# Six projections of two attentions: float32 matmuls from one copy of x in place of split products

## The chip, the core and the metric

The kernel runs on one core of a Trainium2 chip, as one launch. The metric is the device time of an execution in microseconds (us), the median of several runs. Before the change three runs took 1376.7, 1376.79 and 1377.83 us. The engines are TensorE (PE in the profile, its weight loads PEld), VectorE (DVE), ScalarE (ACT), GpSimd (POOL) and SyncE (SP), whose queue issues nearly all weight transfers.

## What is computed

Two transformer blocks on 256 tokens of 1024 features. Only the start of the first block matters here: the input is normalised and modulated, multiplied by one wide weight matrix, and the columns are shared out between a softmax attention ("fox") and a delta-rule recurrence ("rwkv").

```python
mod = silu(c) @ ada_w + ada_b                    # six vectors: sh1, sc1, g1, sh2, sc2, g2
h = rms_norm(x, norm1_g) * (1 + sc1) + sh1       # the modulated x: 256 x 1024
z = h @ w_in
y_fox  = fox_mixer(z[..., :FOX_COLS], ...)       # q, k, v, g: 512 columns each, 8 heads, and small gates
y_rwkv = rwkv7_mixer(z[..., FOX_COLS:], ...)     # r, k, v: 512 columns each, and low-rank parts
x = x + g1 * (concat(y_fox, y_rwkv) @ w_out)
# then a mixture of 64 experts (6 a token), and a second block of four mixers, cross attention and a gated FFN

def rwkv7_mixer(zr, mu, ...):
    zr = zr + mu * (shift_prev(zr) - zr)         # every column mixed with the token before
    r, k, v, wd, ad, gd = split_cols(zr, RWKV_SPLITS)
    ...
    o = wkv7_scan(r, decay, k, v, -kk, kk * a)   # a 64x64 state for each of 8 heads
```

## The kernel before the change

Activations lie feature-major: 128 partitions, and for each of 8 chunks of 128 features the 256 tokens. A projection of 256 output features ("step" below) is one weight tile `w` of 128x2048 (1 MB) and, for each of two halves of 128 outputs, eight products that accumulate in PSUM over the eight chunks.

There are two ways to make such a step. `gemm` (line 358) multiplies float32 weights and a float32 operand directly: 16 matmuls, each of which the profile shows as two records. `gemm3` (line 372, through `mm3`, line 383) first splits: a weight piece of 128x512 is cast to the format fp32r (`wh`, line 308 on VectorE or line 310 on ScalarE) and the remainder `wl` is subtracted on GpSimd (line 325), four pieces to a step. The operand is split once, into `xh` and `xl`. Then three fp32r matmuls (`wh` with `xh`, `wh` with `xl`, `wl` with `xh`) stand for each product, 48 to a step, one record each. The table `HD` (line 35) says which of the casts VectorE makes: all of them in the delta rule's steps (streams "0" and "1"), every second one in the other attention's ("g"); ScalarE makes the rest.

`phase_a` (line 520) makes everything up to the experts. Its first loop computes the modulation chunk by chunk (`ada`), writes the modulated x in place into the tiles `x0` and splits it into `xh` and `xl`. In the same loop it already makes four early projections, the delta rule's k among them. Then eight streams, written as generators, are woven together by the string `ORDER` (line 33): each letter advances one stream by a step. "0" and "1" prepare the two halves of the delta rule's heads (`rwkv_prepare`; its projections come from `krv`, k from the early work, r and v by `gemm3`), "g" is `fox_in` twice (four steps a half: k, q, v, g) and then the second block's memory, "a" the rest of the modulation (`po<-w,cz` in the profile, one weight tile and four matmuls a step), "c" the gates, "f" the softmax attention, "r" the recurrence, "w" the output projection.

A scheduler then places the woven instructions in one fixed order for each engine; an engine goes through its own in that order and waits where an operand, or the buffer that it writes, is not ready. Things that bind the steps to each other are:

- the ring of three 1 MB weight slots (`RING`, line 22; `weights`, line 289): a load waits until the tile three loads earlier has been read for the last time, by the last split of a `gemm3` step or by the last matmul of the others;
- two PSUM banks of each kind ("mm" for projections, "ps" for the delta rule), which the evictions on ScalarE and VectorE give back;
- VectorE's order. In the delta rule's preparation it makes the scaled keys (`kk`, `AR`, `BK`), masks the 64x64 blocks that TensorE multiplies from them (`LT<-ps`), then solves the triangular systems row by row (15 rounds of a shuffle, a product `rowj` and a sum `MC`).

`KQVG` is a set of eight 128x512 buffers, empty until `fox_in` of the first half takes four, that of the second half four more; the input x, loaded again for the residual, takes the first four over.

Of the kernel before, what the change touches and what calls it, by code (L numbers as in the profile page):

```python
# [9 lines left out]
F32 = mybir.dt.float32  # L10
# [3 lines left out]
AF = mybir.ActivationFunctionType  # L14
OP = mybir.AluOpType
# [3 lines left out]
T = 256  # L19
# [12 lines left out]
NG = 3  # L32
ORDER = "00a11101a111a0a0aa0gacc0gagagfgrafgragrfagrarfgarfrarafrargfrgrfgrfgrgrgfrgrgfrgfrgrfgrgrfgrgrfgrgfgrfrwrwwwwwww"
ALT = {}
HD = {'0': 1, '1': 1, 'g': 2}
LAG = 2
EP = 0
early_pool = lambda k: EP and k % EP == 0
# [227 lines left out]
class Prog:  # L266
# [242 lines left out]
    def phase_a(self):  # L509
        nc = self.nc  # L510
        ctx = ExitStack()
        with ctx:
# [3 lines left out]
            fb = self.pool("foxA", bufs=1, ctx=ctx)  # L516
# [20 lines left out]
            ps = self.ps("ps")  # L537
# [18 lines left out]
            xh = fb.tile([128, NK, T], F32R, tag="xh", name="xh")  # L556
            xl = fb.tile([128, NK, T], F32R, tag="xl", name="xl")
            gs = fb.tile([128, 8], F32, name="gs1")
            x = lambda k: (xh[:, k, :], xl[:, k, :])
            early, here, sides = [], 0, {1: ("w_misc0", 256, "mm"), 2: ("w_misc1", 128, "mm"), 3: (0, 256, "fx"), 4: (3, 256, "fx")}  # L560

            def products(u, k):
                w, n, ps = u
                wh, wl = (self.sp.tile([128, 4, 128], F32R, tag=t, name=t)[:, :n // 128] for t in self.parts)
                w = w[k // 4][:, k % 4 * n:k % 4 * n + n]
                self.split(wh, wl, w.rearrange("p (c m) -> p c m", m=128), nc.gpsimd if early_pool(k) else None)
                for c in range(n // 128):
                    for i, (a, b) in enumerate(((wh, xh), (wh, xl), (wl, xh))):
                        self.mm(ps[:, T * c:T * c + T], a[:, c, :], b[:, k, :], start=k + c + i == 0, stop=k == NK - 1 and i == 2)

            def load(k):
                n, m, tag = sides[k]
                src = self.a[n] if isinstance(n, str) else self.a["w_in"][n]
                w = [big.tile([128, 4 * m], F32, tag="E", bufs=NE, name="early") for i in range(2)]
                for i in range(2):
                    nc.sync.dma_start(w[i], src[:, 4 * m * i:4 * m * i + 4 * m])
                return w, m, self.ps(tag)

            for k in range(NK + LAG):
                if k == 5:  # L580
                    self.masks()
                if k < NK:
                    w = self.weights(self.a["ada"][k]).rearrange("p (j n) -> p j n", j=8)
                    ps = self.ps(("po", "pt")[k % 2])
                    for j in range(8):
                        self.mm(ps[32 * (j % 4):32 * (j % 4) + 32, :256], self.cz[:, j, :], w[:, j, :], start=j < 4, stop=j >= 4)
                    row = self.wk.tile([128, 256], F32, tag="hk", name="row")
                    nc.scalar.copy(row, ps[:, :256])
                    for i in range(2):
                        self.mm(ps[:, 256 + i:257 + i], row[:, 128 * i:128 * i + 128], self.ones[:, 0:1])  # L590
                    self.ts(gs[:, k:k + 1], ps[:, 257:258], self.par("ada_b", 8 + k), 1.0, OP.add, OP.add)
                    self.tt(self.mod[:, k:k + 1], ps[:, 256:257], self.par("ada_b", k), OP.add)
                    t = x0[k // 2][:, k % 2, :]
                    self.stt(t, t, self.par("n1g", k), rs, OP.mult, OP.mult)
                    self.ts(t, t, gs[:, k:k + 1], self.mod[:, k:k + 1], OP.mult, OP.add)
                    self.split(xh[:, k, :], xl[:, k, :], t)
                if k >= LAG:
                    for u in early:
                        products(u, k - LAG)
                if k in sides:  # L600
                    u = load(k)
                    for i in range(k - LAG + 1):
                        products(u, i)
                    early.append(u)
# [6 lines left out]
            def shifted(dst, i, p=128):  # L611
                def f(ps):
                    self.act(dst, ps[:p], AF.Identity, scale=omu[:p, i:i + 1])
                    self.stt(dst[:, 1:], ps[:p, :T - 1], mu[:p, i:i + 1], dst[:, 1:], OP.mult, OP.add)
                return f
# [17 lines left out]
            def krv(hf, u):  # L633
                t = big.tile([128, 2, T], F32, tag="K", bufs=6, name="krv"[u] + str(hf))
                i = (4, 0, 8)[u] + 2 * hf
                if u == 0:
                    for c in range(2):
                        shifted(t[:, c, :], i + c)(early[2 + hf][2][:, T * c:T * c + T])
                    return t
                self.gemm3(self.weights(self.a["w_in"][3 * hf + u]), 2, x, lambda c, ps: shifted(t[:, c, :], i + c)(ps))  # L640
                return t

            self.keep = big.tile([128, 8, C], BF, tag="keep", name="keep")
# [11 lines left out]
            for hf in range(2):  # L655
# [4 lines left out]
                for c in range(2):  # L660
                    f, o = 128 * c, slice(T * c, T * c + T)
# [9 lines left out]
            def half(hf):  # L671
                halves[hf] = yield from self.rwkv_prepare(big, low, lambda u: krv(hf, u), hf)

            def chain(*g):
                for i in g:
                    yield from i
            def w_out(hf):
# [11 lines left out]
                for u in range(2):  # L689
                    w = (wo[u] if hf else self.weights(self.a["w_out"][u])).rearrange("p (k n) -> p k n", k=4)  # L690
                    for c in range(4):
# [3 lines left out]

            streams = {"0": (half(0), "ps", ""), "1": (half(1), "ps", ""), "c": (self.foxgate(fb, faa), "fx", "f"),
                       "a": (chain(self.ada(1, "po"), self.ada(2, "po")), "fx", "f"),
                       "g": (chain(self.fox_in(fb, x, 0), self.fox_in(fb, x, 1), self.memory(fb)), "mm", "m"),
                       "f": (chain(self.fox(fb, faa, 0, cat), self.fox(fb, faa, 1, cat)), "fx", "f"),
                       "r": (self.rwkv(big, fb, g0, g1, halves, cat), "ps", ""), "w": (w_out(0), "fx", "f")}  # L700
            done = dict.fromkeys(streams, 0)
# [2 lines left out]
            for m in ORDER + "01cagfrw" * 40:  # L704
                if m in ready and not ready[m]():
                    continue
                g, self.tag, self.sfx = streams[m]
                self.alt, self.hd = ALT.get(m, ALTA), HD.get(m, 0)
                done[m] += 100 if next(g, self) is self else 1
# [322 lines left out]
    def fox_in(self, fb, x, hf):  # L1032

        self.kqvg += [[fb.tile([128, 2, T], F32, tag="KQVG", bufs=8, name="f" + n) for n in "kqvg"]]
        for u, t in enumerate(self.kqvg[hf]):
            w = self.weights(self.a["w_in"][6 + 4 * hf + u])
            self.gemm3(w, 2, x, lambda c, ps: self.act(t[:, c, :], ps, AF.Sigmoid if u == 3 else AF.Copy))
            yield

    def fox(self, fb, faa, hf, cat):  # L1040
# [1241 lines left out]
```

## Time and profile before

| | |
|---|---|
| median of three runs | 1376.79 us |
| the profiled execution | 1373.87 us, its span 1372.1 us |
| TensorE busy | 1273.7 us, 93% of the span |
| VectorE, ScalarE, GpSimd busy | 768.6, 648.0, 334.3 us |
| TensorE's granted clock, mean | 0.952 of full speed |
| casts and subtractions of weight splits, whole program | 180 casts on ScalarE, 110.1 us; 205 subtractions on GpSimd, 268.5 us |

A matmul's duration in the profile runs from its issue to its last output, so neighbours overlap; the distance from one start to the next is its price in a full stream. "PEclk" is the share of full clock that was granted to TensorE; its two levels are 1.2 and 2.4 GHz, so 0.5 is all of a stretch at the lower one. Text in brackets behind a row is the engine's idle time just before it and the instruction that ended it.

### The profile page before, as it was taken

How to read it: one execution, taken by the hardware profiler on the slowest of the kernel's cores; microseconds unless marked ns; L12 is line 12 of the kernel's file. 1: busy time of each engine (PE TensorE's matmuls, PEld its weight loads, DVE VectorE, ACT ScalarE, POOL GpSimd, SP SyncE). 2: the span in 40 equal slices, each digit the busy share in tenths (PEclk: the TensorE clock that was granted, in tenths of full speed). 3: DMA queues.
4: the chain of work that ended last, by engine and by line, in shares of the span. 5: the costliest groups of instructions: out<-in, count | busy, mean ns of one | idle time of the engine just before them, and what ended most of it. 6: DMA issues, size and time to landing. Idle time of an engine off the chain costs nothing. (4 is left out here: it accounts for less than half of the span.)

```text
span 1372.1 us, 26977 instructions
## 1 busy us (share of the span) xinstructions
PE 1273.7 (93%) x10110; PEld 908.1 (66%) x10110; DVE 768.6 (56%) x2032; ACT 648.0 (47%) x1313; POOL 334.3 (24%) x291
## 2 busy tenths in 40 slices
PE   5989799999999999999999999999999887999996
PEld 3767676778854444444444444477878767999996
DVE  3679845645775455555555554466535457544445
ACT  2541233234255555565555555544434544455552
POOL 0132551103200000000000000012434721266662
PEclk9989999899999999999999999999898988999998
DMA  9433555222779999999999999652212422344530
GB/s 362 181 125 152 183 217 193 93 77 110 304 285 382 385 389 399 400 385 389 390 387 399 398 395 393 255 203 106 93 62 96 150 110 106 104 179 179 180 128 31
DMA packets 47077, 321.00 MB, mean 234 GB/s; under 512 B 5216, under 2 KB 5856, under 8 KB 9184
## 3 DMA queue, kind: packets, MB, share of 16 engines
q1 hardware_dynamic: 45072, 316.17, 59.4%
q10 hardware_dynamic: 1872, 3.08, 0.7%
q8 instruction: 80, 1.31, 0.4%
q14 instruction: 53, 0.43, 0.1%
HBM read 318.19 MB, written 1.05 MB: 233 GB/s over the span
## 5 line engine op out<-in xcount | busy, mean ns | idle before, releaser
L325 POOL TENSOR_TENSOR wl<-w,wh 128x512 fp32r<-128x512 f32 x205 | 268.5, 1328 | 377.8 <-ACT wh L310 267.6
L1498 ACT COPY second<-w 128x512 f32 x384 | 217.9, 619 | 85.3 <-PE mm L318 59.5
L318 PE MATMUL mm<-xh,wh 128*128 128x256 f32 (+1 forms) x704 | 209.1, 297 | 6.7 <-DVE r L331 3.2
L318 PE MATMUL mm<-xh,wl 128*128 128x256 f32 (+1 forms) x704 | 208.7, 297 | 4.0 <-POOL wl L325 3.5
L318 PE MATMUL mm<-xl,wh 128*128 128x256 f32 (+1 forms) x704 | 206.5, 293 | 0.0
L1498 DVE COPY second<-w 128x512 f32 x384 | 146.2, 427 | 86.0 <-PE mm L318 80.1
L310 ACT CAST wh<-w 128x512 fp32r<-128x512 f32 x180 | 110.1, 620 | 154.6 <-PE mm L318 98.1
L318 PEld LDWEIGHTS mm<-xh,wh 128*128 128x128 f32 (+1 forms) x704 | 140.3, 199 | 16.5 <-issue 4.1
L328 POOL TENSOR_SCALAR PT<-consts,ws 128x256 fp32r<-128x256 f32 x32 | 31.2, 985 | 474.2 <-DVE ws L1454 446.3
L318 PEld LDWEIGHTS mm<-xh,wl 128*128 128x128 f32 (+1 forms) x704 | 140.0, 199 | 8.4 <-POOL wl L325 4.5
L318 PEld LDWEIGHTS mm<-xl,wh 128*128 128x128 f32 (+1 forms) x704 | 140.2, 199 | 2.9 <-issue 2.2
L318 PE MATMUL mm<-w,xg 128*32 128x512 f32 x1024 | 133.7, 594 | 0.0
L318 PE MATMUL mm<-second,xg 128*32 128x512 f32 x1024 | 133.3, 592 | 0.0
L318 PEld LDWEIGHTS mm<-second,xg 128*32 128x32 f32 x1024 | 34.1, 110 | 75.8 <-issue 66.1
L325 DVE TENSOR_TENSOR yl<-mm,yh 128x512 fp32r<-128x512 f32 x64 | 43.9, 690 | 70.9 <-ACT yh L1532 70.9
L318 PEld LDWEIGHTS mm<-w,xg 128*32 128x32 f32 x1024 | 31.6, 110 | 69.2 <-issue 63.1
L318 PE MATMUL mm<-second,hT 128*32 128x512 f32 x512 | 74.9, 594 | 0.0
L318 PE MATMUL mm<-w,hT 128*32 128x512 f32 x512 | 71.3, 603 | 1.5 <-ACT hT L1518 1.5
L318 PE MATMUL ps<-P,hh 128*128 128x256 f32 x256 | 67.7, 295 | 0.1
L318 PE MATMUL ps<-P,hl 128*128 128x256 f32 x256 | 66.2, 286 | 0.0
L1532 ACT CAST yh<-mm 128x512 fp32r<-128x512 f32 x64 | 37.5, 586 | 59.0 <-PE mm L318 58.5
L318 PE MATMUL acc<-PT,yh 128*128 128x256 f32 x256 | 61.5, 287 | 0.2
(644 smaller groups left out, 2556.7 us busy)
## 6 DMA issues: line engine op xcount, KB each, us to landing
w<-in_exp_dram SPq DMA_DIRECT2D x192, 1024.0 KB, 9.2
w<-in_ada_dram SPq DMA_DIRECT2D x24, 1024.0 KB, 5.1
w<-in_ffi_dram SPq DMA_DIRECT2D x22, 1024.0 KB, 5.0
w<-in_w_dram SPq DMA_DIRECT2D x14, 1024.0 KB, 4.8
w<-in_w_in_dram SPq DMA_DIRECT2D x12, 1024.0 KB, 4.9
w<-in_ffo_dram SPq DMA_DIRECT2D x11, 1024.0 KB, 4.9
w<-in_w_out_dram SPq DMA_DIRECT2D x4, 1024.0 KB, 4.9
w<-in_mixout_dram SPq DMA_DIRECT2D x4, 1024.0 KB, 4.9
```

The costliest lines, as they stand in the source:

```text
L310: self.nc.scalar.copy(h, x)
L318: return self.nc.tensor.matmul(o, l, r, start=start, stop=stop, skip_group_check=True).ins
L325: (eng or self.nc.vector).tensor_tensor(out=o, in0=x, in1=y, op=op)
L328: (eng or self.nc.vector).tensor_scalar(out=o, in0=x, scalar1=s1, scalar2=s2, op0=op0, op1=op1)
L1498: c = (nc.scalar.copy if q % 2 else nc.vector.tensor_copy)(s[:, q:q + 1, :], w[:, bass.ds(reg[q], 1), :])
L1532: nc.scalar.copy(yh, ps)
```

## The change

The modulated x is kept in float32, in four tiles `hf32` that take the four `KQVG` buffers which lie empty at that time; the scaling writes it there instead of over `x0`. `xh` and `xl` are still split from it. Six kinds of step lose the split: the delta rule's r and v in both halves (four steps) and the first half of fox's k, q, v and g (four steps) become `gemm` with `h`. The second half of fox keeps `gemm3`, and so do all the later users. With no split left in streams "0" and "1" their entries in `HD` go. The buffers of `KQVG` now go round one turn further: h, first half, second half (over h), reloaded x (over the first half's).

```diff
-HD = {'0': 1, '1': 1, 'g': 2}
+HD = {'g': 2}
...
+            hf32 = [fb.tile([128, 2, T], F32, tag="KQVG", bufs=8, name=f"h{i}") for i in range(4)]
+            h = lambda k: hf32[k // 2][:, k % 2, :]
...
-                    self.ts(t, t, gs[:, k:k + 1], self.mod[:, k:k + 1], OP.mult, OP.add)
-                    self.split(xh[:, k, :], xl[:, k, :], t)
+                    self.ts(h(k), t, gs[:, k:k + 1], self.mod[:, k:k + 1], OP.mult, OP.add)
+                    self.split(xh[:, k, :], xl[:, k, :], h(k))
...
-                self.gemm3(self.weights(self.a["w_in"][3 * hf + u]), 2, x, lambda c, ps: shifted(t[:, c, :], i + c)(ps))
+                self.gemm(self.weights(self.a["w_in"][3 * hf + u]), 2, h, lambda c, ps: shifted(t[:, c, :], i + c)(ps))
...
-                       "g": (chain(self.fox_in(fb, x, 0), self.fox_in(fb, x, 1), self.memory(fb)), "mm", "m"),
+                       "g": (chain(self.fox_in(fb, h, 0), self.fox_in(fb, x, 1), self.memory(fb)), "mm", "m"),
...
-            self.gemm3(w, 2, x, lambda c, ps: self.act(t[:, c, :], ps, AF.Sigmoid if u == 3 else AF.Copy))
+            (self.gemm3 if hf else self.gemm)(w, 2, x, lambda c, ps: self.act(t[:, c, :], ps, AF.Sigmoid if u == 3 else AF.Copy))
```

The scheduler places the instructions anew. From the first step of fox's second half on, TensorE's order is what it was; before that it differs. On GpSimd, in the stretch where the projections are made, the order before was this (`wl<-w,wh` is a subtraction, `Z` a buffer of the recurrence):

```order
L325 TENSOR_TENSOR wl<-w,wh 128x512 x27
L873 MEMSET Z 128x512 x2
L325 TENSOR_TENSOR wl<-w,wh 128x512 x21
L884 MEMSET Z 128x8x32
L325 TENSOR_TENSOR wl<-w,wh 128x512
```

and now it is this:

```order
L875 MEMSET Z 128x512 x2
L325 ISA
L325 TENSOR_TENSOR wl<-w,wh 128x512 x16
L886 MEMSET Z 128x8x32
L325 TENSOR_TENSOR wl<-w,wh 128x512
```

Of 48 subtractions ahead of the second clearing of `Z`, 32 are gone, and the first clearing no longer stands among them.

On VectorE, late in the triangular solver of the delta rule's preparation, stood this (`rowj` and `MC` are the solver's, `fdf` belongs to fox's k, `r_1033<-ps,v_1166` is the product that gives back a "ps" bank of half 0):

```order
L308 CAST wh<-w 128x512
L849 STREAM_SHUFFLE rowj<-MC 128x16x8
L325 TENSOR_TENSOR rowj<-rowj,LD 128x16x8
L325 TENSOR_TENSOR MC<-MC,rowj 128x16x8
L849 STREAM_SHUFFLE rowj<-MC 128x16x9
L325 TENSOR_TENSOR rowj<-rowj,LD 128x16x9
L325 TENSOR_TENSOR MC<-MC,rowj 128x16x9
L849 STREAM_SHUFFLE rowj<-MC 128x16x10
L325 TENSOR_TENSOR fdf<-fk 128x2x255
L328 TENSOR_SCALAR fdf<-fk 128x2
L325 TENSOR_TENSOR rowj<-rowj,LD 128x16x10
L325 TENSOR_TENSOR r_1033<-ps,v_1166 128x512
```

and now, five rounds of the solver later:

```order
L851 STREAM_SHUFFLE rowj<-MC 128x16x14
L325 TENSOR_TENSOR rowj<-rowj,LD 128x16x14
L325 TENSOR_TENSOR MC<-MC,rowj 128x16x14
L325 TENSOR_TENSOR fdf<-fk 128x2x255
L328 TENSOR_SCALAR fdf<-fk 128x2
L851 STREAM_SHUFFLE rowj<-MC 128x16x15
L325 TENSOR_TENSOR r_941<-ps,v_1026 128x512
```

No cast stands between the rounds any more, and the product has moved from the tenth round into the fifteenth.

On TensorE, where the blocks `AR,BK` of half 0 are multiplied, stood this:

```order
L318 MATMUL ps<-consts,k_710 64x128 x8
L318 MATMUL mm<-xh,wh 128x256
L318 MATMUL mm<-xl,wh 128x256
L318 MATMUL mm<-xh,wl 128x256
L318 MATMUL mm<-xh,wh 128x256
L318 MATMUL mm<-xl,wh 128x256
L318 MATMUL ps<-AR,BK 64x128 x16
L318 MATMUL mm<-xh,wl 128x256
L318 MATMUL mm<-xh,wh 128x256
L318 MATMUL mm<-xl,wh 128x256
L318 MATMUL mm<-xh,wl 128x256
L318 MATMUL ps<-AR,BK 64x128 x16
```

and now (`h_138` is a tile of the float32 x):

```order
L318 MATMUL ps<-consts,k_714 64x128 x8
L318 MATMUL po<-w,cz 32x512
L318 MATMUL ps<-AR,BK 64x128 x32
L318 MATMUL po<-w,cz 32x512 x3
L318 MATMUL mm<-h_138,w 128x256 x2
```

The blocks of half 0 now stand together, without pieces of a projection between them, and two whole projection steps follow.

## Rows read from the trace of the kernel before

**Rows 1.** Busy us of each engine by stretch; then granted clock, DMA share, GB/s.

```profile
62.40:173.00 110.60, 93.90 (x702) 73.95 (x701) 94.56 (x210) 34.70 (x68) 46.53 (x36) 0.88 0.43 154
173.00:336.40 163.40, 155.20 (x1465) 122.65 (x1464) 88.13 (x257) 54.32 (x134) 38.96 (x32) 0.92 0.36 128
```

**Rows 2.** What TensorE waited for, 62.4 to 173 us: total, times, longest.

```profile
PE ps L818 <- DVE r L325: 4.8, 1, 4.8
PE mm L318 <- DVE r L331: 3.2, 1, 3.2
PE mm L318 <- POOL wl L325: 2.9, 3, 1.1
PE mm L318 <- DVE wh L308: 1.7, 3, 0.8
PE ps L318 <- DVE AR L325: 1.4, 1, 1.4
PE ps L318 <- DVE LT L325: 1.1, 2, 0.8
PE ps L318 <- ACT wa L337: 0.6, 1, 0.6
PE ps L318 <- ACT sgw L337: 0.6, 1, 0.6
```

**Rows 3.** The four stretches with TensorE at the lower clock, columns as in Rows 1.

```profile
70.00:74.00 4.00, 4.00 (x20) 3.71 (x19) 1.99 (x3) 3.94 (x6) 2.06 (x1) 0.57 0.00 0
93.00:101.00 8.00, 8.00 (x30) 6.41 (x31) 6.25 (x23) 1.07 (x3) 1.44 (x2) 0.50 0.11 47
121.00:128.00 7.00, 6.19 (x54) 5.39 (x49) 6.29 (x14) 0.00 (x0) 0.19 (x1) 0.54 0.01 2
148.00:152.50 4.50, 4.49 (x22) 4.49 (x23) 3.06 (x12) 1.76 (x3) 0.56 (x1) 0.53 0.00 0
```

**Rows 4.** TensorE in order of time: fp32r products at full clock (start, us).

```profile
79.80 0.28 PE L318 MATMUL mm<-xh,wh 128*128 128x256 f32 x1
...
80.15 0.28 PE L318 MATMUL mm<-xh,wh 128*128 128x256 f32 x1
```

**Rows 5.** TensorE in order of time: a float32 gemm of the expert stage.

```profile
367.44 7.12 PE L318 MATMUL mm<-xgain,w 128*128 128x257 f32 x32
374.40 0.31 PE L318 MATMUL ps<-rmb,rbef 128*128 128x64 bf16 x5
```

**Rows 6.** Weight splits by form, 62.4 to 173 us: busy, mean ns | idle before.

```profile
L325 POOL TENSOR_TENSOR wl<-w,wh 128x512 fp32r<-128x512 f32 x34 | 46.6, 1384 | 81.3 <-DVE wh L308 70.7 <-DVE lb L325 4.6 <-PE mm L318 1.6
L308 DVE CAST wh<-w 128x512 fp32r<-128x512 f32 x25 | 12.7, 520 | 8.1 <-PE mm L318 3.6 <-POOL wl L325 3.5 <-issue 1.0
```

**Rows 7.** VectorE's solver in order of time, and GpSimd at that time.

```profile
132.32 2.55 POOL L325 TENSOR_TENSOR wl<-w,wh 128x512 fp32r<-128x512 f32 x2 [1.06 <-DVE MC L325]
...
132.58 1.09 DVE L325 TENSOR_TENSOR rowj<-rowj,LD 128x32 f32<-128x32 f32 x1
...
135.22 0.21 DVE L325 TENSOR_TENSOR rowj<-rowj,LD 128x48 f32<-128x48 f32 x1
```

**Rows 8.** VectorE in order of time: the delta rule's half 1 ends, half 0 begins.

```profile
114.88 0.68 DVE L325 TENSOR_TENSOR r<-ps,v 128x512 f32<-128x512 f32 x1
...
117.96 1.76 DVE L325 TENSOR_TENSOR AR<-r,Ep 128x512 f32<-128x512 f32 x1
```

**Rows 9.** A weight load of the ring, what released it, and times to landing.

```profile
127.81 1.33 POOL L325 TENSOR_TENSOR wl<-w,wh 128x512 fp32r<-128x512 f32 x1 [6.96 <-DVE wh L308]
...
129.17 0.33 SPq L293 DMA_DIRECT2D w<-in_w_in_dram  x1
...
w<-in_w_in_dram SPq DMA_DIRECT2D x12, 1024.0 KB, 4.9
```

**Rows 10.** Weight loads of an fp32r and of a float32 gemm.

```profile
79.81 0.19 PEld L318 LDWEIGHTS mm<-xl,wh 128*128 128x128 f32 x1
...
L318 PEld LDWEIGHTS mm<-xgain,w 128*128 128x128 f32 x32 | 6.1, 189 | 0.9
```

## The prediction, on record before the run

> **What bounds the kernel now.** The diff touches the weave of streams between the end of the early projections and the first step of fox's second half, so I first looked at where that stretch lies in TensorE's order of time: from 62.4 us (the first `po<-w,cz` after the early products) to 173.0 us (the first split product of fox's second half), 110.6 us. Then I read the engines by stretch. In it TensorE is busy for 93.9 us and VectorE for 94.6 [rows 1]: neither waits much, and both serve each other. In the 163 us behind it TensorE is busy for 155.2, VectorE for only 88.1, and TensorE's order there is the same before and after; so what the stretch gains or loses moves all that follows by as much, if nothing else sets the pace there.
>
> TensorE is without work for 110.6 - 93.9 = 16.7 us. The waits say on whom [rows 2]: 4.6 us directly on a split (2.9 on GpSimd's subtraction, 1.7 on a cast), 10.5 us on VectorE's queue (4.8, 3.2, 1.4 and 1.1), 1.2 us on ScalarE, the rest 0.4. The second loss is the clock. Four stretches run at 0.50 to 0.57 of full clock [rows 3]; three of them follow a wait of 3.2, 1.4 and 4.8 us, the first follows the alternation of small low-rank products with waits on ScalarE. What they cost is their length times the missing share: 4.0 x 0.43 = 1.7, 8.0 x 0.50 = 4.0, 7.0 x 0.46 = 3.2 and 4.5 x 0.47 = 2.1, together 11.0 us.
>
> **TensorE's price of the change.** A split step is 48 products. At full clock one begins (80.15 - 79.80) / 3 = 0.117 us after the other [rows 4], so a step is 5.6 us. A float32 gemm of the same shape (one column more) stands in the expert stage: its 32 records take 374.40 - 367.44 = 6.96 us, 0.2175 each [rows 5]. Sixteen matmuls are 32 records, 7.0 us. Eight steps go from 44.9 to 55.7 us: 10.8 us more, all on TensorE. The weight loads are in that price: a load takes 0.19 us for fp32r and for float32 alike [rows 10], and float32 products start 0.2175 us apart with their loads beneath them. The Trainium skill, "TensorE: Matmul & The Clock Gate", section "Weight-path perf modes", speaks against the change: float32 weights are left out of the fast load that other types get. The trace does not agree that this costs anything here, since both loads are equally long; if each of 256 loads stood bare, it would be 256 x 0.19 = 48.6 us more.
>
> **What goes.** GpSimd loses 32 of the 34 subtractions in the stretch, 1.38 us each: 44 of its 46.6 us. VectorE loses 16 casts of the delta rule's steps and 8 of fox's, 24 x 0.52 = 12.5 us [rows 6]; ScalarE loses 8. VectorE also loses company. While GpSimd subtracts, a solver product of 128x32 takes 1.09 us; without, the larger one of 128x48 takes 0.21 [rows 7]. Some twenty-five of VectorE's instructions in the stretch are longer by such a 0.9 us, counted in its order of time, some for splits that stay: an estimate of 18 to 22 us that go. VectorE's 94.6 us thus fall to about 62, and it stops being the engine that holds the others up. The nearest example is the AR product of half 0: three casts stand ahead of it and it takes 1.76 us itself, so that it ends at 119.72 where the string ahead of it ended at 115.56 [rows 8]. Without these it needs about 2.2 us for the same rows instead of 4.2.
>
> **What remains late.** Without waits and at full clock the stretch is 110.6 - 16.7 - 11.0 + 10.8 = 93.7 us. I then followed the new order of TensorE and VectorE from wait to wait:
> - the 1.2 us on ScalarE stay: its table loads and sigmoids ahead of the low-rank products are not touched;
> - the 4.6 us on splits go entirely;
> - the squares of the keys come after only nine float32 matmuls of v, where 42 split products stood ahead of them, so TensorE gets there sooner; but VectorE's scan ahead of them is no longer behind four casts. I get 0.3 us, and 0.3 more at the transposes of the square roots behind them;
> - the blocks AR,BK of both halves hang on VectorE's string of scaled keys, in which no cast stood; it moves forward as a whole. The two halves cost 0.7 and 1.0 us;
> - the product that frees a bank for half 0's transposes was the wait of 4.8 us. It now stands in the solver's fifteenth round instead of the tenth. The rounds, at undisturbed durations, take about 14 us, and begin as soon as half 0's last block is masked. In that time TensorE has two whole float32 steps (14.0 us) and some 2.6 us of small work. The two arrive within a microsecond: 0.6 us.
>
> With 0.1 for a last eviction the waits come to 4.2 us. They can be 1.3 (ScalarE alone) or, if VectorE is as late as before at two of its places, 8.
>
> For the clock I keep what stands on causes that remain: the first stretch (1.7), and the third (3.2), since the 64x64 blocks and transposes there still come in one piece. The two that follow the 3.2 and 4.8 us waits go. That is 4.9 us; the ends are 1.7 and 11.0.
>
> **Edits that cost nothing.** The scaling writes to another tile with the same one instruction, and the orders of VectorE and ScalarE up to the early projections' end are unchanged but for names. Weight slots come free later: a split step gave its slot back with its last subtraction (the load at 129.17 follows the subtraction that ended at 129.14), a float32 step with its last matmul; landing takes 4.9 us [rows 9]. A load has at least one 7.0 us step between its release and its first matmul, so it lands in time. The closest is the second split step of fox's second half: its slot is freed when the last float32 step ends; 4.9 us to land, about 2.0 for a first cast and subtraction, against 5.6 us of the first split step and two small pieces of 1 us. If that cover fails it costs under 2 us. The second half's tiles take over h's buffers; their evictions follow the last float32 matmul on TensorE anyway.
>
> **Sum.** 93.7 + 4.2 + 4.9 = 102.8 us instead of 110.6: 7.8 us less. Against the profiled execution of 1373.87 us (span 1372.1) that is 1366.1; its time lies 2.9 us under the median of the runs, so I put the difference on the median: 1376.79 - 7.8 = 1369.0 us. With the inner ends (waits 1.3 to 6, clock 1.7 to 7.0) the stretch is 96.7 to 106.7 us, and the time 1362.9 to 1372.9.
>
> **Rivals.**
> - *The clock stays low.* Float32 products follow small ones and waits as before: 93.7 + 8 + 11.0 = 112.7, 2.1 us more than now, 1378.9 us. For it speaks that three of four low stretches begin after small work that stays; against it that the two longest waits lose their cause.
> - *The delta rule's own chain holds the pace.* TensorE's longer steps deliver r and v later, VectorE's string starts later, and the waits move rather than go. Then nothing is won back: plus 10.8, 1387.6 us, slower. It decides from the point where waits and clock together give back less than 10.8 of their 27.7 us. For it: VectorE is as busy as TensorE. Against it: some 30 us of VectorE's time in the stretch go with the splits.
> - *More comes back.* The clock holds and only ScalarE's waits remain: 93.7 + 1.3 + 0 = 95.0, 15.6 us less, 1361.2.
> - *Given back later.* The early start of fox's second half meets late weights and splits, 3 us over its four steps: 1372.0.
> - *Bare weight loads.* Each load delays its product instead of lying beneath the one before: plus 10.8 and 48.6, 1436 us. Against it [rows 5, 10]. It is what the rule on fast loads in the Trainium skill's page "TensorE: Matmul & The Clock Gate" could make of it.
>
> **Chances.** The forecast has 0.60, low clock 0.11, delta rule's chain 0.10, more 0.11, given back 0.07, bare loads 0.01. Runs of this kernel differ by up to 0.1%; 0.2%, 2.8 us, is what a measurement can tell from no change. Forecast, more and given back are faster: 0.78. Low clock is within: 0.11. The other two are slower: 0.11. The range from 1361 to 1379 us holds forecast, low clock, given back and half of the larger gain, some 0.83. The forecast's own is 1363 to 1373.
>
> **What would show it.** In the profile after, `mm<-h,w` would have 256 records that start 0.217 us apart at full clock; the first split product of fox's second half would start at about 165 us instead of 173; VectorE would be busy for 60 to 66 us up to there; the waits on `wl` and `wh` would be gone and no wait on VectorE over 1.5 us left; the four low stretches would be two. Everything behind would lie earlier by the same amount, the first expert's products too. I am wrong if float32 records start further apart than 0.22 us at full clock, if a wait of several us appears at the key squares or the solver, or if the gain at 165 us is gone by 336.

## The result, and the profile after

The changed kernel takes 1359.46 us (median of 4 runs, 1355.08 to 1362.05); the kernel before, run beside it, 1376.74 (4 runs, 1368.83 to 1377.83). The recorded ratio is 0.9896 with a 95% interval of 0.986 to 0.9932; it is not the quotient of the two medians, which is 0.9875, and the ratios below differ from theirs in the same way by up to 0.005. The profiled execution of after took 1362.05 us, its span 1360.3, against 1373.87 and 1372.1 before: 11.8 us less.

The stretches first, columns as in [rows 1]: from the first `po<-w,cz` after the early products to the first split product of fox's second half, and as much again behind it as [rows 1] shows.

```profile
60.99:155.10 94.11, 92.73 (x573) 65.30 (x573) 62.53 (x187) 32.06 (x62) 2.96 (x3) 1.00 0.48 179
155.10:318.50 163.40, 156.91 (x1429) 124.30 (x1426) 79.65 (x239) 50.28 (x128) 33.51 (x28) 0.86 0.35 122
```

The stretch lasts 94.1 us where it lasted 110.5 (its end, the first split product, stands at 172.92 us in the kernel before; [rows 1] is cut at 173.0). TensorE is busy for 1.2 us less although its work at full clock is 10.8 us more, because its granted clock is 1.00 throughout where it was 0.88; VectorE falls from 94.6 to 62.5 us. Behind it the clock goes the other way, from 0.92 to 0.86.

What TensorE waited for in the stretch, all of it, against [rows 2]:

```profile
PE ps L318 <- DVE LT L325: 0.6, 2, 0.3
PE ps L820 <- DVE r L325: 0.3, 1, 0.3
PE ps L493 <- DVE nw L331: 0.2, 1, 0.2
```

Nine kinds of wait (the eight of [rows 2] and one of 0.2 us) are three; the 4.8 us on `r` are 0.3. TensorE in order of time shows the price of the float32 steps (start, us), as [rows 4, 5] did:

```profile
113.28 14.08 PE L318 MATMUL mm<-h,w 128*128 128x256 f32 x64
127.29 0.64 PE L318 MATMUL po<-w,cz 128*32 128x512 f32 x4
...
131.03 0.66 PE L820 MATMUL ps<-consts,kk 128*128 128x128 f32 x4 [0.31 <-DVE r L325]
```

Sixty-four records take 14.01 us, 0.2189 each. The other groups, by form, in the stretch (busy us, mean ns): GpSimd's subtractions against [rows 6], and on VectorE the product of [rows 8]:

```profile
L325 POOL TENSOR_TENSOR wl<-w,wh 128x512 fp32r<-128x512 f32 x3 | 3.7, 1270 | 108.1 <-ACT wh L310 108.1
...
L325 DVE TENSOR_TENSOR AR<-r,Ep 128x512 f32<-128x512 f32 x2 | 1.4, 688 | 0.0
```

and the same product in the kernel before:

```profile
L325 DVE TENSOR_TENSOR AR<-r,Ep 128x512 f32<-128x512 f32 x2 | 2.4, 1219 | 0.0
```

The mean of the two is 688 instead of 1219 ns, for the same instructions on the same data: one of them took 1.76 us before [rows 8]. Last, where the gain stands farther back, the first expert's products, at 367.44 us in [rows 5]:

```profile
357.95 0.81 PE L318 MATMUL mm<-xgain,w 128*128 128x257 f32 x3
```

Fox's second half starts 172.9 - 155.1 = 17.8 us earlier, of which 1.4 us lie ahead of the stretch (that part ends between 59.8 and 66.3 us over the kernels of this study). At the first expert's products 9.5 us are left, at the end 11.8. Eight microseconds are given back between 155 and 358 us, and they are in TensorE's busy time. From the end of the stretch to those products, in after and then in the kernel before:

```profile
155.12:357.95 202.83, 192.47 (x1675) 157.29 (x1673) 105.27 (x328) 65.23 (x156) 49.66 (x41) 0.88 0.43 160
172.92:367.44 194.52, 184.26 (x1675) 149.75 (x1673) 107.59 (x330) 67.40 (x159) 51.26 (x42) 0.93 0.45 166
```

The same 1675 matmuls keep TensorE busy for 8.2 us longer, at a clock of 0.88 instead of 0.93; its waits there come to 10.3 us, against 10.1 before.

### The profile page after: what moved, and what is told of

Read it like the earlier page. It is cut to its first block, busy times and chain, and to the rows that moved or that the text cites. A ratio compares the mean times of both kernels' runs of the same rounds, so it can differ in the third digit from the quotient of the medians.

```text
span 1360.3 us, 26588 instructions
## 1 busy us (share of the span) xinstructions
PE 1276.8 (94%) x9982; PEld 903.8 (66%) x9982; DVE 733.9 (54%) x2008; ACT 643.5 (47%) x1305; POOL 290.9 (21%) x259
## 5 line engine op out<-in xcount | busy, mean ns | idle before, releaser
L325 POOL TENSOR_TENSOR wl<-w,wh 128x512 fp32r<-128x512 f32 x173 | 224.7, 1318 | 410.6 <-ACT wh L310 380.5
L318 PE MATMUL mm<-xh,wh 128*128 128x256 f32 (+1 forms) x576 | 169.6, 295 | 1.8 <-ACT xh L310 1.8
L318 PE MATMUL mm<-xh,wl 128*128 128x256 f32 (+1 forms) x576 | 169.6, 295 | 0.5 <-DVE wl L325 0.5
L318 PE MATMUL mm<-xl,wh 128*128 128x256 f32 (+1 forms) x576 | 168.3, 292 | 0.0
L310 ACT CAST wh<-w 128x512 fp32r<-128x512 f32 x172 | 105.2, 620 | 127.4 <-PE mm L318 89.4
L318 PEld LDWEIGHTS mm<-xh,wh 128*128 128x128 f32 (+1 forms) x576 | 114.2, 198 | 6.4 <-ACT xh L310 2.1
L318 PEld LDWEIGHTS mm<-xl,wh 128*128 128x128 f32 (+1 forms) x576 | 114.0, 198 | 2.3 <-issue 1.7
L318 PEld LDWEIGHTS mm<-xh,wl 128*128 128x128 f32 (+1 forms) x576 | 113.8, 198 | 1.9 <-DVE wl L325 0.8
```

Of the source, the lines that this page charges most:

```text
L310: self.nc.scalar.copy(h, x)
L318: return self.nc.tensor.matmul(o, l, r, start=start, stop=stop, skip_group_check=True).ins
L325: (eng or self.nc.vector).tensor_tensor(out=o, in0=x, in1=y, op=op)
```

## The experiments

Theory A, formed from [rows 6, 7] and the profile after: GpSimd's subtractions make VectorE's instructions beside them longer, and TensorE waits, and loses clock, on strings of those (a string is a row of small VectorE instructions, each of which needs the one before, with a product of TensorE at its end). Its rivals: VectorE's casts, or the splits as work, whoever does it. Eleven kernels ran, each timed against the kernel before on the same chip (its medians there 1370.3 to 1371.6 us).

**e0_again**: the changed kernel once more, beside the next three. It took 1358.6 us (ratio 0.987, 0.9817 to 0.9923). Its expectation:

> The changed kernel again, unaltered, for a second profile and more times. In the first profile the stretch from the first modulation product behind the early projections to the first split product of fox's second half took 94.1 us at full clock, and the 163.4 us of work behind it ran at a mean clock of 0.86 where it was 0.92 before. My theory: the gain of the stretch (16.5 us) is partly given back behind it by stretches at the lower clock, and these fall differently from one execution to the next. Expected: the stretch 94 to 95 us again; the clock of the 163 us behind it anywhere from 0.84 to 0.94, and the span shorter when it is higher, about 1.6 us for 0.01. Rival: what is given back is fixed by the new order; then the same low stretches come back at the same places and the span is 1360 again. Median 1359 to 1363 on either.

The stretch was 94.0 us at clock 1.00, with the same three waits, and the clock behind it 0.89. The result repeats. The expectation's theory does not do so well: for a clock of 0.89 instead of 0.86 it asks for a span some 5 us shorter, and the span is 1.6 us shorter (1358.7). Its rival, that the new order fixes what is given back, fits better: in the second and the fourth 10 us behind the stretch the clock is 0.83 and 0.66, in the first profile 0.83 and 0.67, and in the kernel before 1.00 in both.

**e4_subs_back, e3_casts_back, e5_both_back.** Float32 products stay as changed; beside each float32 step stand instructions whose output nobody reads: subtractions `v - v` of weight pieces on GpSimd, casts on VectorE, or both, as many as the change removed.

```diff
+    def idle_split(self, w, casts, subs):
+        wv = w.rearrange("p (k n) -> p k n", k=NK)
+        for j in range(4):
+            v = wv[:, j % 2 * 4:j % 2 * 4 + 4, 128 * (j // 2):128 * (j // 2) + 128]
+            if j % 4 < casts:
+                self.nc.vector.tensor_copy(self.sp.tile([128, 4, 128], F32R, tag="wh", name="wh"), v)
+            if j % 4 < subs:
+                self.tt(self.sp.tile([128, 4, 128], F32R, tag="wl", name="wl"), v, v, OP.subtract, self.nc.gpsimd)
...
+                self.idle_split(w, 0, 4)      # e4; e3: (w, 4, 0) for r, v and (w, 2, 0) for fox; e5: both
```

> The changed kernel with 32 subtractions put back on GpSimd, four of 128x512 for each of the eight float32 steps, on the weight tile itself and into a scratch buffer that nobody reads; nobody on TensorE or VectorE waits for them, and the order of these two is that of the changed kernel row for row. Theory A (GpSimd's subtractions make VectorE's two-input products longer, and that alone was most of VectorE's delay): VectorE is busy for about 20 us more in the stretch, TensorE waits 3 to 8 us more, the stretch takes 98 to 104 us, the kernel 4 to 10 us longer than the changed one. Theory B (VectorE's delay came from the casts and from waits for the splits themselves): VectorE's busy time grows too, but TensorE's waits stay under 2 us; the kernel within 2 us of the changed one.

e4 took 1372.83 us, ratio 1.002 (0.9984 to 1.0057): the gain is gone, and 14 us are more than the 4 to 10 that theory A expected. The stretch too is longer than its 98 to 104 us, though VectorE's busy time grows by less than the 20 us expected. Its stretch and its waits there:

```profile
62.38:173.90 111.52, 102.45 (x574) 70.98 (x573) 76.41 (x187) 31.95 (x62) 39.01 (x37) 0.91 0.40 151
```

```profile
PE ps L503 <- DVE nw L331: 3.2, 1, 3.2
PE ps L318 <- DVE LT L325: 2.9, 2, 2.7
PE ps L832 <- DVE r L325: 2.3, 1, 2.3
PE ps L318 <- DVE AR L325: 0.3, 1, 0.3
```

(This execution, span 1379.6 us, is one of e4's longer ones.) No wait names GpSimd, since nobody uses what it makes; TensorE and VectorE do the same instructions in the same order as in after, over the whole program. Yet VectorE is busy 13.9 us longer, TensorE waits 8.7 us instead of 1.1, and its busy time is 9.7 us longer at a clock of 0.91. VectorE and GpSimd in order of time in e4 show how:

```profile
142.01 1.08 DVE L325 TENSOR_TENSOR MC<-MC,rowj 128x192 f32<-128x192 f32 x1
...
143.13 0.44 DVE L863 STREAM_SHUFFLE rowj<-MC 128x208 f32<-128x208 f32 x1
...
144.26 1.09 DVE L325 TENSOR_TENSOR MC<-MC,rowj 128x208 f32<-128x208 f32 x1
...
146.30 0.39 DVE L325 TENSOR_TENSOR MC<-MC,rowj 128x224 f32<-128x224 f32 x1
```

```profile
140.72 4.40 POOL L325 TENSOR_TENSOR wl<-w 128x512 fp32r<-128x512 f32 x4 [14.01 <-DMA w<-in_w_in_dram]
```

and two of the same forms in after, where GpSimd is idle:

```profile
L325 DVE TENSOR_TENSOR MC<-MC,rowj 128x192 f32<-128x192 f32 x1 | 0.4, 357 | 0.0
L851 DVE STREAM_SHUFFLE rowj<-MC 128x208 f32<-128x208 f32 x1 | 0.4, 439 | 0.0
```

While GpSimd's four subtractions run (140.72 to 145.12), VectorE's sums of two operands take 1.08 and 1.09 us instead of 0.36 to 0.38; the next one after them is back at 0.39, and the shuffle, which reads one operand, takes 0.44 beside a subtraction or without. The Trainium skill, "SBUF — State Buffer", section "Who interferes with whom", says that a VectorE instruction with two operands in SBUF contends with a GpSimd instruction that reads SBUF, and one with a single operand outside certain fast modes does not. These rows agree.

> The changed kernel with 24 casts of 128x512 put back on VectorE, four for each float32 step of the delta rule and two for each of fox's, into a scratch buffer that nobody reads. 24 x 0.43 us is 10 us more of VectorE's time. Theory A (contention with GpSimd was most of it): TensorE still waits under 3 us, the stretch 94 to 97 us, the kernel within 3 us of the changed one. Theory B (casts in VectorE's queue): the stretch 98 us or more, the kernel 4 us or more longer.

e3 took 1360.67 us, ratio 0.991 (0.9873 to 0.9947). Its stretch:

```profile
60.59:154.99 94.40, 92.69 (x573) 65.34 (x573) 70.51 (x211) 32.33 (x62) 2.71 (x3) 1.00 0.49 179
```

VectorE is 8.0 us busier and nothing else moves: 24 casts fit into its idle time.

> The changed kernel with both put back: 24 casts on VectorE and 32 subtractions on GpSimd that nobody waits for. What is left of the change then is that TensorE makes 256 float32 records in place of 384 split products (10.8 us more) and no longer waits for a split. If VectorE's relief is what pays (theories A or B), VectorE is as busy as before the change, 90 us or more, the stretch takes 102 to 110 us and the kernel is within 5 us of the one before. If the gain comes from TensorE's own side (no direct waits on splits, 4.6 us, and denser work that holds the clock), the stretch stays under 98 us and the kernel within 4 us of the changed one.

e5 took 1376.22 us, ratio 1.0034 (1.0005 to 1.0063); the stretch of the profiled execution was 108.9 us at a clock of 0.95, with 11.3 us of waits, and VectorE is busy for 91.5 us, as the expectation's first case had it; the time is 5.3 us above the kernel before, where it allowed 5. The casts, too, get longer beside the subtractions: 843 ns in the mean, 418 in e3. Whether the casts add to the subtractions here can't be told: the two intervals overlap.

**e1_delta_only and e2_fox_only**: one half of the change each.

```diff
-                        "g": (chain(self.fox_in(fb, h, 0), self.fox_in(fb, x, 1), self.memory(fb)), "mm", "m"),
+                        "g": (chain(self.fox_in(fb, x, 0), self.fox_in(fb, x, 1), self.memory(fb)), "mm", "m"),
...
-            (self.gemm3 if hf else self.gemm)(w, 2, x, lambda c, ps: self.act(t[:, c, :], ps, AF.Sigmoid if u == 3 else AF.Copy))
+            self.gemm3(w, 2, x, lambda c, ps: self.act(t[:, c, :], ps, AF.Sigmoid if u == 3 else AF.Copy))
```

That is e1; e2 has instead the delta rule's line back, `gemm3` with `x`, and its casts on VectorE.

> Only the delta rule's four steps (r and v of both halves) are float32 products; the first half of fox's k, q, v and g is split again, so 16 of the 32 subtractions and 8 casts of VectorE come back and TensorE saves 5.4 us against the changed kernel. Theory A (GpSimd's subtractions lengthen what VectorE does beside them; each pair of VectorE and GpSimd instructions costs alike): about half of the gain goes, the stretch lasts 99 to 104 us, the waits on VectorE add up to 3 to 6 us, and the time is 1362 to 1368 where the kernel before takes 1371. Rival (what matters is that no split stands between the delta rule's own pieces of VectorE): the gain stays, TensorE's 5.4 us come on top, the stretch is 89 to 95 us and the time 1353 to 1358.

> Only the first half of fox's k, q, v and g is float32 products; the delta rule's r and v are split again with their 16 casts on VectorE and 16 subtractions on GpSimd. Theory A: as with the other half alone, the stretch lasts 99 to 104 us and the time is 1362 to 1368. Rival (only the delta rule's own steps matter): VectorE's string is as late as before, the stretch is 112 to 116 us (110.5 and 5.4 us more of TensorE) and the time 1371 to 1376.

e1: 1361.45 us, ratio 0.9887 (0.9841 to 0.9934). e2: 1374.48 us, ratio 1.0013 (0.9982 to 1.0044). Their stretches, e1 and then e2:

```profile
59.83:156.68 96.85, 89.68 (x637) 65.79 (x637) 75.84 (x195) 34.70 (x68) 23.39 (x20) 0.98 0.49 177
```

```profile
64.57:170.97 106.40, 99.68 (x638) 74.35 (x637) 78.71 (x201) 32.06 (x62) 26.89 (x21) 0.87 0.43 159
```

Neither expectation held. I had let theory A say that each half is worth half; but 16 subtractions cost less where they stand in e1 than in e2, beside the delta rule's own steps. Each half saves TensorE 5.4 us of work against after; with these added, the stretch is 96.85 + 5.4 - 94.1 = 8.2 us longer than in after for e1 and 106.4 + 5.4 - 94.1 = 17.7 us for e2 (estimates, from one profile each). The rival's time fits e2 and its stretch does not (106.4, not 112 to 116), and e1 lies between the two. The number of subtractions alone does not set the price; that the strings on which they fall do is the likely reading, but e2 also has eight casts more on VectorE, which e3 alone speaks against. In e1 TensorE's waits are 7.0 us and it still keeps a clock of 0.98; in e2 they are about as long and the clock is 0.87. So the low clock is not a fixed multiple of the waits.

**e6_before_no_gpsimd**: the kernel before, with every split product, but in streams 0, 1 and g ScalarE casts and VectorE subtracts. **e8_second_half_on_vector**: the changed kernel with the same edit for the splits that remain in g (16 of fox's second half among them).

```diff
-ALT = {}
-HD = {'0': 1, '1': 1, 'g': 2}
+ALT = {'0': 0, '1': 0, 'g': 0}    # e6, on the kernel before: 0 puts the subtraction on VectorE
+HD = {}
...
-HD = {'g': 2}
+ALT = {'g': 0}                    # e8, on the changed kernel
+HD = {}
```

> The kernel before, with all its split products, but in the streams 0, 1 and g all casts are made by ScalarE and all subtractions by VectorE, none by GpSimd. TensorE does 10.8 us less than in the changed kernel. Theory A (GpSimd's subtractions cost VectorE its time, not the splits as such): a subtraction on VectorE takes 0.69 us (a neighbouring split there shows 686 ns), 34 of them 23.5 us; VectorE's busy time in the stretch is 94.6 - 12.7 (casts) - 18 (contention) + 23.5 = 87 us, the stretch 92 to 100 us and the time 1355 to 1364 without a float32 product. Rival (VectorE's work as such is the bound, whoever makes it long): at 87 us VectorE stays as busy as TensorE, the waits on VectorE stay at 10 us or more, the stretch 106 to 114 us and the time 1368 to 1376.

> The changed kernel, but the splits that stay in stream g (fox's second half and the memory's) are cast by ScalarE and subtracted by VectorE. The stretch up to fox's second half is as it was, 94 us. Behind it 16 or more subtractions leave GpSimd. Theory A: VectorE's small steps (the nw roots, on which TensorE waited 3.1 us) lose their company; the 163 us of work behind the stretch take 2 to 6 us less, at a granted clock of 0.90 or more, and the time is 1353 to 1358 where the changed kernel takes 1359. Rival (behind the stretch VectorE has room, 80 of 163 us busy, and the low clock there has other causes): within 1.5 us of the changed kernel, and 3 us slower if VectorE's subtractions stand ahead of the roots.

e6: 1353.66 us, ratio 0.9822 (0.9772 to 0.9872): faster than before without one float32 product, and 1.3 us below the range of theory A. TensorE waits on VectorE for 2.5 us there, so the rival, with 10 or more, falls. (e6 moves the casts as well; in e3, and in e11 below, where casts alone move, the time stays.) Its stretch:

```profile
66.26:163.98 97.72, 91.73 (x702) 71.61 (x701) 79.41 (x214) 45.05 (x90) 0.00 (x0) 0.90 0.50 179
```

e8: 1342.53 us, ratio 0.9769 (0.9725 to 0.9812), 17 us below the changed kernel where 1 to 6 were expected. Its 163.4 us behind the stretch, and the first expert's products:

```profile
154.80:318.20 163.40, 159.34 (x1549) 128.43 (x1546) 92.26 (x273) 65.33 (x155) 17.22 (x16) 0.97 0.44 158
```

```profile
337.58 1.25 PE L318 MATMUL mm<-xgain,w 128*128 128x257 f32 x5
```

The clock there is 0.97 instead of 0.86, and the experts start 20.4 us earlier than in after. The first fall of the clock behind the stretch in after can be followed row by row. VectorE, then GpSimd and TensorE in after:

```profile
163.18 1.41 DVE L328 TENSOR_SCALAR nw<-nx 128x8 int32<-128x8 int32 x3
```

```profile
160.79 3.77 POOL L325 TENSOR_TENSOR wl<-w,wh 128x512 fp32r<-128x512 f32 x3 [2.17 <-ACT wh L310]
```

```profile
164.29 0.28 PE L318 MATMUL mm<-xh,wh 128*128 128x256 f32 x1
165.72 0.38 PE L493 MATMUL fx<-consts,nw 128*4 128x128 f32 x2 [1.15 <-DVE nw L331]
...
168.13 0.42 PE L318 MATMUL mm<-xl,wh 128*128 128x256 f32 x1
168.34 0.41 PE L318 MATMUL mm<-xh,wl 128*128 128x256 f32 x1
```

and in e8, VectorE and TensorE:

```profile
162.86 0.32 DVE L328 TENSOR_SCALAR nw<-nx 128x8 int32<-128x8 int32 x3
```

```profile
164.44 0.38 PE L493 MATMUL fx<-consts,nw 128*4 128x128 f32 x2
...
167.02 0.28 PE L318 MATMUL mm<-xl,wh 128*128 128x256 f32 x1
167.13 0.28 PE L318 MATMUL mm<-xh,wl 128*128 128x256 f32 x1
```

The first three small steps of a reciprocal root take 1.41 us beside GpSimd's subtractions (three from 160.79 to 164.56) and 0.32 without. (They read one tile each, as the shuffle above does, and get longer all the same; why, no run shows.) TensorE therefore waits 1.15 us in after and not at all in e8; behind that wait products start 0.21 us apart where e8 goes on at 0.117. The granted clock of those three microseconds in after, columns as in [rows 1], is the lower of its two levels:

```profile
167.60:170.60 3.00, 3.00 (x15) 2.99 (x15) 0.87 (x2) 0.62 (x1) 0.55 (x1) 0.52 0.65 202
```

The kernel before has the same root, the same subtractions and no such wait. GpSimd, VectorE and TensorE there:

```profile
176.84 5.18 POOL L325 TENSOR_TENSOR wl<-w,wh 128x512 fp32r<-128x512 f32 x4 [1.63 <-DVE wh L308]
```

```profile
181.83 0.36 DVE L328 TENSOR_SCALAR nw<-nx 128x8 int32<-128x8 int32 x3
```

```profile
183.32 0.38 PE L493 MATMUL fx<-consts,nw 128*4 128x128 f32 x2
```

Its subtractions end at 182.02, as the root begins, and the clock stays at 1.00; e0 repeats the wait of after (1.15 us, at 166.32). So in after the root stands beside GpSimd's subtractions, where it did not stand before. The next low stretch is not explained by its wait. The next root meets subtractions in both kernels, in after and then in before:

```profile
184.50 0.38 PE L493 MATMUL fx<-consts,nw 128*4 128x128 f32 x2 [1.96 <-DVE nw L331]
```

```profile
200.42 0.38 PE L493 MATMUL fx<-consts,nw 128*4 128x128 f32 x2 [1.83 <-DVE nw L331]
```

and for the 6 us behind it the clock is at its lower level in after and full in before:

```profile
184.70:190.70 6.00, 6.00 (x24) 4.94 (x23) 2.16 (x5) 2.14 (x4) 1.50 (x1) 0.51 0.17 71
```

```profile
200.60:206.60 6.00, 6.00 (x46) 5.42 (x45) 3.19 (x5) 2.15 (x4) 1.29 (x1) 1.00 0.29 101
```

**e11_casts_on_scalar**: e8's other edit alone (`HD = {}`): ScalarE casts, GpSimd still subtracts.

> The changed kernel with one of the two edits of e8: ScalarE makes all casts of stream g, but GpSimd keeps the subtractions. Theory A (GpSimd's subtractions, not VectorE's casts, cost the time behind the stretch): the time stays at 1356 to 1362, the granted clock of the 163 us behind the stretch at 0.86 to 0.90 and the waits on the nw roots at about 3 us. Rival (it was the casts standing in VectorE's order, or the order of the instructions that their move brings): the time is that of e8, 1340 to 1347, and the clock behind 0.95 or more.

1358.62 us, ratio 0.9907 (0.9873 to 0.9942): the time of after. Its waits and stretch behind 156 us:

```profile
PE fx L493 <- DVE nw L331: 4.1, 2, 2.1
PE po L447 <- DVE fo L325: 1.9, 1, 1.9
```

```profile
156.18:319.58 163.40, 156.28 (x1442) 123.62 (x1439) 78.92 (x231) 57.19 (x140) 34.83 (x29) 0.90 0.35 125
```

The casts' move alone gains nothing, so it is the subtractions' engine that e8 gained by, and theory A holds behind the stretch too.

**e9_delta_only_no_gpsimd** (e1 with e8's edit) and **e10_all_on_vector** (e8 with the constants `ALTA`, `ALT1`, `ALTC`, `ALTF` at 0 and `ALTX` at 1, so that VectorE makes the other stages' 149 subtractions too).

> As e8, but only the delta rule's r and v are float32 products; the first half of fox's projections is split again, cast by ScalarE and subtracted by VectorE. TensorE saves 5.4 us against e8, VectorE gets 16 subtractions of 0.69 us, 11 us, more (64 to 75 of 90 us). Theory A: the waits stay under 3 us, the stretch is 88 to 93 us and the time 1336 to 1342 where e8 takes 1342.5. Rival (VectorE's work as such holds TensorE up): waits of 5 us or more at the key squares or the solver, as with GpSimd's 16 subtractions in e1, a stretch of 95 to 98 us and a time of 1343 to 1347.

> As e8, and the 149 subtractions of weight splits that are left on GpSimd in the other stages are made by VectorE too (0.69 us each, 103 us; VectorE would be busy for 840 of 1333 us). Theory A, if it holds beyond this stretch: the waits on VectorE in the second block get shorter and the time is 1325 to 1340. Rival (where VectorE has no string that TensorE waits for, GpSimd's help is worth more than its contention): 1345 to 1360.

e9: 1342.57 us, ratio 0.9798 (0.9757 to 0.9838). Its first split step of fox's second half begins at 149.6 us, a stretch of 89.3, in which TensorE is without work for 1.6 us, as theory A said; but the median is no better than e8's, and lies between the times of theory A (1336 to 1342 us) and of the rival (1343 to 1347). The profiled executions differ behind the first block's experts (from one and the same product 477.8 us to the end in e9, 467.1 in e8), where both do the same work, so 5 us of gain can't be told from the scatter there. e10: 1328.58 us, ratio 0.9698 (0.9668 to 0.9727), within theory A's 1325 to 1340 and the fastest kernel of the study, 31 us below the changed one. Its sign is missing, though: from the end of the first block's experts on, TensorE's waits on VectorE come to 21.2 us in e8 and in e10 alike, and what got shorter is its busy time, 427.6 to 420.4 us. So how the gain arises in the other stages is not shown.

## Why the prediction was right, and where it was not

The direction and the mechanism were right; the predicted 1369.0 us is 9.5 above the median measured, which lies 1.5 us under the lower end of the stated range (1361 to 1379); the recorded ratio, 0.9896 of 1376.79, gives 1362.5, inside it. The gain was foretold too small: 7.8 us are a ratio of 0.9943, outside the interval. The 0.1% by which runs were said to differ came from three runs; on the chips of the experiments the kernel before took 1361.0 to 1381.9 us. By its steps:

- **TensorE's price**: 0.2189 us a record where I took 0.2175. Base without waits and at full clock: 93.7 predicted; TensorE is busy for 92.7. Right. The weight loads cost nothing bare, and that rival falls.
- **What VectorE gains**: 62.5 us busy, "about 62" predicted. Right, and e4 and e3 show that the part with company, not the casts, is what counts for the time. Of the 32.0 us that VectorE lost, e3 puts 8.0 back, e4 13.9 and e5, with both, 28.9.
- **What remains late**: 4.2 us predicted, 1.1 measured. The wait at the solver is 0.31 (0.6 predicted), that at the key squares is gone, the one at their roots 0.2 (0.3 predicted), the two at the masked blocks come to 0.6 (1.7 predicted), and the 1.2 us on ScalarE, which I had called untouched, are gone. One working was wrong without harm: the `AR` product of half 0 ends 3.9 us after the string ahead of it, not 2.2, since VectorE now idles 1.67 us for an `r` that ScalarE delivers later; nobody waits for it.
- **The clock** is the term most mis-sized: I kept two of four low stretches, 4.9 us, and none remained. I had tied them to small products, which are still there; the low stretches went when the waits did, though no run shows that each hangs on its wait. With the waits this is 8.0 of the 8.7 us by which the stretch came out shorter than 102.8. The rival *more comes back* (95.0 us, 1361.2) is what happened inside it.
- **"Moves all that follows by as much"** is the step that failed. I took TensorE's unchanged order behind 173 us for unchanged time, without looking at GpSimd there: when both move, its subtractions fall on other of VectorE's instructions, as the first root behind the stretch shows. Of 17.8 us 8.3 went by the first expert's products, as lower clock: TensorE's busy time for the same 1675 matmuls is 8.2 us longer, its waits 0.2 us. The prediction's own clause "if nothing else sets the pace there" is where it would have had to look. *Given back later* was therefore right in kind and wrong in cause: no weight or split was later, as TensorE waits for neither from 155 to 230 us, and up to the experts for 1.8 us on splits, against 2.6 before. A term too small and one left out, in opposite directions, brought the sum nearer than its parts; that much of it was luck.
- **Delta rule's chain** and **low clock in the stretch** did not happen here; e4 shows what decides. With GpSimd busy as before, float32 steps and all, the stretch is 111.5 us and the time that of before.

What stays open: why the clock behind the stretch is 0.86 and 0.89 in two executions of after and 0.92 in before, with the same splits there (its first fall was followed to a wait that before does not have, the next stands behind a wait that before has too); and what float32 is worth by itself. Without GpSimd in these streams it still brings 1353.7 to 1342.5 us, so the splits cost something as VectorE's and TensorE's order too, although e3 finds the casts free. What e6 loses at a clock of 0.90 wasn't followed further.

## What to carry to other kernels

Before removing work from a bound engine, look at what an idle-looking helper does beside it: GpSimd's subtractions cost VectorE, and TensorE behind it, more here than the help was worth, though few waits name GpSimd (2.9 of 16.7 us in the kernel before, none in e4). Idle copies of the suspected instructions, with outputs that nobody reads, tell this from the order and from the work itself. And unchanged instruction order behind an edit is no proof of unchanged time: small strings that meet the same helper, and the clock after their waits, must be read there too.

## What the runs showed of the hardware

- Thirty-two 128x512 subtractions on GpSimd, 36.5 us in all and read by nobody, cost the program 14 us (1358.6 to 1372.8).
- A subtraction of that size takes 1.3 us on GpSimd (149 of them in e8, mean 1320 ns) and 0.69 on VectorE (184 of them in e10, median 692 ns), so the helper was slower than the engine it helped and held it up besides.
- At full clock 64 float32 records in a row take 0.219 us each, an fp32r product 0.117. A float32 product is two records, 0.438 us; the three fp32r products in its place are 0.351 us.
